# New piece orders, a later place for the first negated copies, and bank drains on VectorE in the units made ahead, in a two-layer hybrid decoder trunk

## The chip, the cores and the metric

The kernel runs on one core of one Trainium2 chip. The metric is the device time of one execution in microseconds; the times of the kernel before and after are medians over several runs. One profiled execution of each kernel gives the trace from which the lines below are taken. Engines are named as in the profile: PE is TensorE (matrix products), PEld its weight loads, DVE is VectorE, ACT is ScalarE, POOL is GpSimd and SP is SyncE, which issues most DMAs.

## The reference

Two decoder layers on 256 tokens of width 2048, all in float32. Cut to what matters:

```python
D_MODEL, SEQ, DEPTH, D_FF = 2048, 256, 2, 8192

def hybrid_layer(x, ...):
    h = rms_norm(x, attn_norm)
    proj = h @ w_in                     # 2048 x 6160: g_q, g_k, g_v, g_gate, g_lr, s_q, s_k, s_v
    log_a = log_sigmoid(g_lr @ w_gate_up + b_gate) / 16
    o_gla = gla_chunked(g_q, g_k, g_v, log_a)            # 8 heads, chunks of 64
    o_gla = rms_norm(o_gla) * silu(g_gate)
    o_sb = stick_breaking_attention(rms_norm(s_q), rms_norm(s_k), s_v)   # 8 heads of 128
    o_sb = rms_norm(o_sb)
    x = x + concatenate([o_gla, o_sb]) @ w_o             # 2048 x 2048
    hm = rms_norm(x, mlp_norm)
    up = square(relu(hm @ w_up))                         # 2048 x 8192
    return x + up @ w_down                               # 8192 x 2048
```

Nearly all of the work is in the products with `w_in`, `w_o`, `w_up` and `w_down`, which are read from DRAM once each. The change touches how these products are ordered and how their results leave the accumulators.

## The kernel before

**Products from high and low parts.** TensorE multiplies a rounded format (`F32R`), so a float32 weight is split: ScalarE rounds it to a high part (`whi`, line L1098), VectorE subtracts that from the weight for the low part (`wlo`, L1102), and every product is three matmuls (`product`, L1231, L1234, L1235): high by high, high by low, low by high. The activations are split in the same way beforehand.

**Units, pieces, steps, banks.** A unit is a product with 2048 rows and 1024 columns of weights. Its rows are cut into 8 pieces of 256 rows, j = 0 to 7; the weights of one piece are one load of 1 MB by SyncE into a `raw` slot (`load`). The unit's order is a list of piece numbers, one number a step: a table such as `EACH` holds the list, the pieces done in the "fast" way and the two "added" pieces. A fast piece has four steps of 6, 6, 6 and 3 matmuls: it forms the 2 x 2 block product with seven products in place of eight, for which VectorE forms sums of weight blocks (`ts`, and sums in place in `raw`, all L876, the line of the helper `combine`). A plain piece has two steps of 12 matmuls. An added piece has two steps of 12, too, but its parts come by DMA: GpSimd issues a load that rounds on its way (`chi`, L1059), ScalarE writes the negated copy of it (`dlo`, L1063, in `negated`), and GpSimd issues a second load that adds the weights to that copy (L1066), which leaves the low part. A unit with four fast pieces has 180 matmuls of 512 columns. Its sums are built in the eight PSUM banks 1 to 8 (tiles `m__...`): in the fast steps 2 and 3, then 5 and 7, then 1 and 6, then 4; in the other steps 2 and 4 with 3 and 8. So banks 5, 7, 1 and 6 are finished with the last fast step, the other four only at the unit's end.

**Slots.** The opening list has six `raw` slots (`FIRST_RAWS`), each later one three (`RAWS`). A load waits until the slot's previous piece has been read for the last time.

**Lists.** The work stands in three planned lists, each followed by work with an order of its own:
- the opening list (`l = -1`): three units made ahead for layer 0's attention, `iv`, `ik`, `iq` (`AHEAD`), ahead of which stands a small opening product (L632, with `copy_first`, L922, that takes its result out of two banks);
- layer 0's list: a gate product, two output units (`o`), sixteen MLP units (four times two `up`, two `down`), and `iv`, `ik`, `iq` for layer 1;
- layer 1's list: gate, two output units, sixteen MLP units.

Ahead of layer 0's and of layer 1's list stands that layer's attention; its first product is the one of L630 to L632 with weights split in L611 and L613, whose first accumulator `acc` takes two banks.

**What sets the order.** `Plan` gets one entry per instruction with its engine, an assumed length, what it depends on and, for loads, an assumed time to landing (`lag`). TensorE's entries stand as the order tables have them; due times for all others follow backwards from them, and a list schedule made with these numbers fixes the program order of ScalarE and VectorE. On the chip each engine works through that order from the front: an instruction that waits holds up all behind it.

**Negated copies at the start.** `rounded` makes the entries of an added piece. For the first three (`CAST`) in the opening list, an entry `held_tile` (L1054) takes the tile by a write of one column, then the load L1059 is issued. The entry `held_tile` has no dependency.

**Tails.** `up_tail` empties the banks of `up` units and of `iv`, `ik`, `iq`. Bank 1 is copied by ScalarE to `box[0]`; VectorE makes `dw` = bank 6 - bank 1, then `y(1, 0)` = bank 5 + `dw`, then `dw` = bank 7 + `dw`; these are the sums. After the last step `half` adds banks 2 and 3 to `y(0, 0)` and `y(1, 0)` on VectorE; banks 4 and 8 are first copied by ScalarE (L1391) into `y(0, 1)` and `y(1, 1)`; VectorE then adds bank 5 once more to the copy of bank 8, and `dw` to both. `relu` (L1410) scales the four results; for `iv`, `ik`, `iq` it is a copy with a factor. `free` holds, for each bank, the entries after which the next unit may write to it.

Of the kernel before, what the change touches and what calls it, by code (L numbers as in the profile page):

```python
# [22 lines left out]
EACH = [0, 0, 1, 1, 1, 2, 7, 3, 3, 3, 3, 2, 5, 5, 5, 5, 4, 1, 6, 6, 6, 4, 6, 7], FAST, (2, 4)  # L23
FEWER = [0, 0, 1, 2, 7, 4, 1, 1, 1, 6, 7, 6, 6, 6, 2, 3, 3, 3, 3, 5, 4, 5], (1, 3, 6), (2, 4)
LATER = [0, 4, 0, 5, 5, 3, 5, 5, 4, 3, 3, 2, 1, 1, 3, 1, 1, 2, 6, 6, 6, 6, 7, 7], FAST, (2, 4)
FAST_OF = {"sxh": (0, 1, 3, 5, 6), "sx": (0, 1, 3, 5, 6)}
TWO_WAYS = (("sxh", 0), ("sx", 0))
O0 = [4, 5, 7, 4, 6, 6, 0, 0, 0, 7, 1, 0, 1, 1, 1, 5, 2, 2, 2, 2, 3, 3], (0, 1, 2), (5, 7)
O1 = [4, 6, 4, 1, 1, 2, 1, 5, 1, 2, 0, 0, 2, 2, 0, 5, 0, 3, 6, 3, 7, 7], (0, 1, 2), (5, 6)
# [3 lines left out]
    ("up", 0): ([2, 5, 5, 5, 5, 1, 1, 1, 1, 2, 0, 0, 0, 3, 4, 0, 3, 3, 3, 6, 4, 6, 6, 6, 7, 7], (0, 1, 3, 5, 6), (2, 4)),  # L33
    ("up", 0, 0): ([0, 0, 3, 4, 3, 3, 1, 3, 4, 1, 1, 1, 5, 5, 2, 5, 5, 6, 6, 2, 6, 6, 7, 7], FAST, (2, 4)),
    ("up", 1): ([7, 7, 5, 5, 4, 5, 5, 1, 1, 1, 2, 3, 1, 3, 3, 3, 4, 6, 6, 6, 6, 0, 2, 0], FAST, (2, 4)),
    ("down", 0): ([0, 0, 1, 1, 1, 3, 4, 1, 3, 5, 3, 3, 4, 5, 5, 5, 2, 6, 6, 6, 6, 7, 7, 2], FAST, (2, 4)),
    ("down", 1): ([7, 7, 3, 3, 4, 3, 3, 5, 5, 5, 4, 5, 1, 1, 1, 1, 0, 0, 2, 0, 0, 6, 6, 6, 6, 2], (0, 1, 3, 5, 6), (2, 4)),
# [137 lines left out]
def trunk_kernel(  # L175
# [275 lines left out]
    def forms(op, i, t, tag):  # L451
# [21 lines left out]
        def high():  # L473
            if e:
# [5 lines left out]
                elif keep:  # L480
                    op.x[i] = act_tile(F32R, (P, 4, 2, P))
                else:
                    op.x[i] = tmp(tag, [P, 3, 2, P], F32R, bufs=len(FAST))
# [375 lines left out]
    def ordered(l, units, hT, rst, ug, gates_t, mixed=None, ons=None):  # L859
# [116 lines left out]
        def turned(n, h2, m, op, key, ll, sums=False):  # L976
# [4 lines left out]
            if sums and i in (FAST if op is hT else FAST_OF["sxh"]):  # L981
# [60 lines left out]
        def rounded(u, j, s):  # L1042
# [27 lines left out]
            if l < 0 and len(chi) < CAST:  # L1070
                first = add("ACT", 0.2, held_tile)
# [167 lines left out]
        def bk(m):  # L1239
            return lambda: banks[m]  # L1240
# [116 lines left out]
        def up_tail(u):  # L1357
# [9 lines left out]

            def new_dw():
# [15 lines left out]
            def half(h, p):  # L1384
                box["r", h] = []
                for tt, m in enumerate(((2, 4), (3, 8))[h]):
                    before = p[m]
                    if tt:
# [7 lines left out]
                    if m == 8:  # L1396
# [569 lines left out]
```

## Time and profile before

| what | value |
|---|---|
| three runs | 2145.78, 2146.07, 2139.18 us |
| median | 2145.78 us |
| the profiled execution | 2145.65 us, of which the trace spans 2144.0 us |
| mean granted TensorE clock of that execution | 0.996 |
| PE, DVE, ACT, POOL busy | 99%, 90%, 70%, 13% |
| DMA over the span | 497.16 MB, 232 GB/s |

The time of an execution is that of the whole run on the device; the span is the part that the trace covers, first to last instruction. The share of busy time counts an engine's own instructions. In the lists of waits the row `A <- B` means that an instruction of A stood idle until B released it; a bracket behind a row of the timeline gives the idle time right ahead of it and what ended it. Names such as `m__230_1143` are tiles, the last number counting through the program.

### The profile page before, as it was taken

How to read it: one execution, taken by the hardware profiler on the slowest of the kernel's cores; microseconds unless marked ns; L12 is line 12 of the kernel's file. 1: busy time of each engine (PE TensorE's matmuls, PEld its weight loads, DVE VectorE, ACT ScalarE, POOL GpSimd, SP SyncE). 2: the span in 40 equal slices, each digit the busy share in tenths (PEclk: the TensorE clock that was granted, in tenths of full speed). 3: DMA queues.
4: the chain of work that ended last, by engine and by line, in shares of the span. 5: the costliest groups of instructions: out<-in, count | busy, mean ns of one | idle time of the engine just before them, and what ended most of it. 6: DMA issues, size and time to landing. Idle time of an engine off the chain costs nothing.

```text
span 2144.0 us, 28336 instructions
## 1 busy us (share of the span) xinstructions
PE 2117.9 (99%) x10040; PEld 1762.7 (82%) x10040; DVE 1936.9 (90%) x2658; ACT 1509.6 (70%) x2044; POOL 279.1 (13%) x394
## 2 busy tenths in 40 slices
PE   8999999999999999999999999999999999999998
PEld 6878888888888888888888888888888888888887
DVE  5887868999999999999998786699999999999998
ACT  6666667777677777668776575677776776786775
POOL 0110001111111111111111000011111111111110
PEclk9999999999999999999999999999999999999999
DMA  8765348788988988987988553678889888889886
GB/s 304 215 192 184 124 136 251 223 251 244 260 258 240 273 255 231 275 261 227 260 252 260 158 173 118 212 220 243 255 253 254 253 259 249 250 256 255 250 246 197
DMA packets 160691, 497.16 MB, mean 232 GB/s; under 512 B 10682, under 2 KB 19458, under 8 KB 160548
## 3 DMA queue, kind: packets, MB, share of 16 engines
q1 hardware_dynamic: 100900, 319.16, 41.3%
q0 software_dynamic: 59648, 176.18, 37.0%
q8 instruction: 79, 1.29, 0.2%
q14 instruction: 64, 0.52, 0.1%
HBM read 493.20 MB, written 2.10 MB: 231 GB/s over the span
## 4 chain that ended last, share of the span: by engine, by line
PE 91%; DVE 3%; ACT 3%; DMA 2%; issue 1%; POOL 0%; ACTq 0%; DVEq 0%
PE acc L630 3%; PE acc L632 3%; PE acc L631 3%; DMA raw<-in_w_in_dram 1%; DVE wlo L1102 1%; ACT whi L611 0%; DMA raw<-in_w_o_dram 0%; ACT whi L1098 0%; DMA chi<-in_w_in_dram 0%; PE ps L1903 0%; DVE wlo L613 0%; PE ps L1896 0%; DVE act L876 0%; PE ps L741 0%; PE ps L1853 0%
## 5 line engine op out<-in xcount | busy, mean ns | idle before, releaser
L1102 DVE TENSOR_TENSOR wlo<-raw,whi 128x1024 fp32r<-128x1024 f32 (+1 forms) x697 | 749.7, 1081 | 75.3 <-ACT whi L1098 41.2
L1098 ACT ACTIVATE whi<-raw 128x1024 fp32r<-128x1024 f32 (+1 forms) x697 | 648.9, 947 | 212.6 <-DVE raw L876 77.8
L1063 ACT ACTIVATE dlo<-chi 128x1024 fp32r<-128x1024 f32 x168 | 177.7, 1058 | 102.1 <-DMA chi<-in_w_in_dram 8.8
L1098 ACT ACTIVATE whi<-ts 128x1024 fp32r<-128x1024 f32 x177 | 187.3, 1058 | 70.0 <-DVE ts L876 33.9
L876 DVE TENSOR_TENSOR ts<-raw 128x1024 f32<-128x1024 f32 x177 | 215.5, 1218 | 11.3 <-DMA raw<-in_w_in_dram 8.6
L1102 DVE TENSOR_TENSOR wlo<-ts,whi 128x1024 fp32r<-128x1024 f32 x177 | 215.3, 1216 | 1.8 <-ACT whi L1098 1.7
L630 PE MATMUL acc<-whi,act 128*128 128x512 f32 (+2 forms) x384 | 142.4, 371 | 4.2 <-DVE act L876 4.2
L611 ACT ACTIVATE whi<-raw 128x1024 fp32r<-128x1024 f32 (+2 forms) x98 | 88.6, 908 | 69.7 <-PE acc L632 66.5
L632 PE MATMUL acc<-whi,act 128*128 128x512 f32 (+2 forms) x384 | 137.7, 359 | 0.0
L631 PE MATMUL acc<-wlo,act 128*128 128x512 f32 (+2 forms) x384 | 137.5, 358 | 0.0
L613 DVE TENSOR_TENSOR wlo<-raw,whi 128x1024 fp32r<-128x1024 f32 (+2 forms) x98 | 100.6, 1031 | 34.8 <-ACT whi L611 34.6
L876 DVE TENSOR_TENSOR raw<-raw 128x512 f32<-128x512 f32 x177 | 121.1, 684 | 1.8
L876 DVE TENSOR_TENSOR raw<-ts,raw 128x512 f32<-128x512 f32 x177 | 120.7, 682 | 0.1
L1059 POOL DMA_DIRECT2D chi<-in_w_up_dram x64 | 38.1, 595 | 515.0 <-PE m__2883_13592 L1235 34.8
L1059 POOL DMA_DIRECT2D chi<-in_w_down_dram x64 | 41.6, 650 | 424.6 <-PE m__914_4357 L1235 22.1
L630 PEld LDWEIGHTS acc<-whi,act 128*128 128x128 f32 x384 | 73.4, 191 | 17.1 <-DVE act L876 5.0
L1066 POOL DMA_DIRECT2D dlo<-in_w_down_dram x64 | 65.3, 1020 | 151.9 <-ACT dlo L1063 123.5
L632 PEld LDWEIGHTS acc<-whi,act 128*128 128x128 f32 x384 | 73.2, 191 | 10.4
L631 PEld LDWEIGHTS acc<-wlo,act 128*128 128x128 f32 x384 | 73.3, 191 | 8.9 <-DVE wlo L613 0.2
L1410 ACT ACTIVATE act<-act,st 128x512 f32<-128x512 f32 x88 | 62.3, 717 | 19.1 <-DVE act L876 18.6
L1066 POOL DMA_DIRECT2D dlo<-in_w_up_dram x64 | 57.9, 905 | 54.8 <-ACT dlo L1063 54.0
L492 DVE TENSOR_TENSOR act<-t,act 128x512 fp32r<-128x512 f32 x94 | 63.6, 682 | 0.0
(4536 smaller groups left out, 5809.3 us busy)
## 6 DMA issues: line engine op xcount, KB each, us to landing
raw<-in_w_up_dram SPq DMA_DIRECT2D x96, 1024.0 KB, 6.8
raw<-in_w_down_dram SPq DMA_DIRECT2D x96, 1024.0 KB, 8.3
raw<-in_w_in_dram SPq DMA_DIRECT2D x72, 1024.0 KB, 7.0
chi<-in_w_up_dram POOLq DMA_DIRECT2D x64, 512.0 KB, 5.2
dlo<-in_w_up_dram POOLq DMA_DIRECT2D x64, 512.0 KB, 7.7
chi<-in_w_down_dram POOLq DMA_DIRECT2D x64, 512.0 KB, 6.1
dlo<-in_w_down_dram POOLq DMA_DIRECT2D x64, 512.0 KB, 8.0
raw<-in_w_o_dram SPq DMA_DIRECT2D x24, 1024.0 KB, 7.7
```

What stands on the lines that cost most here:

```text
L492: nc.vector.tensor_tensor(d[:, :, 1, :], src, f32(d[:, :, 0, :]), ALU.subtract)
L611: newest["hi"] = nc.scalar.activation(h, r, AF.Copy).ins
L613: newest["lo"] = nc.vector.tensor_tensor(lo[:, q : q + step, :width], r, f32(h), ALU.subtract).ins
L630: nc.tensor.matmul(o, xh[:, sl], whi[:, j, :width], start=first, stop=False)
L631: nc.tensor.matmul(o, xh[:, sl], wlo[:, j, :width], start=False, stop=False)
L632: st["mm"] = nc.tensor.matmul(o, xl[:, sl], whi[:, j, :width], start=False, stop=last).ins
L876: nc.vector.tensor_tensor(dst, a, b, op)
L1059: nc.gpsimd.dma_start(flat("h"), src)
L1063: nc.scalar.activation(box["l"], f32(box["h"]), AF.Copy, scale=-1.0)
L1066: nc.gpsimd.dma_start(flat("l"), src, accum_op=ALU.add)
L1098: nc.scalar.activation(box["h"][:, :n], src(), AF.Copy)
L1102: nc.vector.tensor_tensor(box["l"][:, :n], src(), f32(box["h"][:, :n]), ALU.subtract)
```

## The change

It has three parts.

1. All order tables have new lists: of the units made ahead (`EACH` in the opening list; `FEWER` and `LATER` in layer 0's), of the output units (`O0`, `O1`), and of `up` and `down` (`OWN`). The sets of fast and added pieces stay as they are in each. `FAST_OF` gets an entry for `ht` with the value that was used for it before.
2. `held_tile`, the entry ahead of each of the first three casting loads, depends on `before[2]`, one of the five entries that stand for the opening product. That makes `Plan` take these loads, and the negations behind them, as later.
3. In `up_tail`, units made ahead (`not into`) no longer have ScalarE's copies of banks 4 and 8 (two instructions of L1391 less in each of the six units). Bank 7 + `dw` goes straight to `y(0, 1)` in place of `dw`; a new sum right behind it makes `y(1, 1)` = bank 5 + `y(0, 1)`, with the second read of bank 5; banks 4 and 8 are added to these by VectorE from PSUM, bank 4 only after that new sum. `dw` is given back after its last use among the sums. For `up` units only the order of two operands changes.

TensorE has 9826 instructions in both programs, the same of each kind, and VectorE 2660; ScalarE has 2002 in place of 2014. GpSimd's DMAs keep their number; of the 64 casting and 64 adding loads of `w_down`, 16 and 16 change from 512 columns of two row blocks to 1024 columns of one, and 4 and 4 of the 24 and 24 of `w_in` the other way.

```diff
-EACH = [0, 0, 1, 1, 1, 2, 7, 3, 3, 3, 3, 2, 5, 5, 5, 5, 4, 1, 6, 6, 6, 4, 6, 7], FAST, (2, 4)
+EACH = [7, 7, 1, 1, 0, 1, 2, 5, 2, 5, 5, 3, 5, 3, 3, 4, 6, 1, 6, 6, 6, 3, 4, 0], FAST, (2, 4)
-O1 = [4, 6, 4, 1, 1, 2, 1, 5, 1, 2, 0, 0, 2, 2, 0, 5, 0, 3, 6, 3, 7, 7], (0, 1, 2), (5, 6)
+O1 = [4, 5, 4, 2, 2, 2, 2, 6, 1, 1, 0, 0, 1, 1, 0, 0, 6, 5, 7, 7, 3, 3], (0, 1, 2), (5, 6)
...
             if l < 0 and len(chi) < CAST:
-                first = add("ACT", 0.2, held_tile)
+                first = add("ACT", 0.2, held_tile, before[2])
...
+            def dw():
+                return box["w"]
...
                 c = box["c"] = add("ACT", A1, copy, p[1])
                 w = add("DVE", V1, new_dw, c, p[6], take=1, sure=1)
-                a = vector(y(1, 0), bk(5), lambda: box["w"], w, p[5])
-                b = vector(lambda: box["w"], bk(7), lambda: box["w"], w, a, p[7])
+                a = vector(y(1, 0), bk(5), dw, w, p[5])
+                b = vector(dw if into else y(0, 1), bk(7), dw, w, a, p[7])
+                box["s"] = (w, b, a, b)
                 free.update({1: [c], 6: [w], 5: [a], 7: [b]})
-                box["s"] = (w, b, a, b)
+                if not into:
+                    b.give = 1
+                    box["s"] = (w, b, a, vector(y(1, 1), bk(5), y(0, 1), b, p[5]))
+                    free[5] = [a, box["s"][3]]
...
                 for tt, m in enumerate(((2, 4), (3, 8))[h]):
-                    before = p[m]
-                    if tt:
+                    before = [p[m], box["s"][3] if m == 4 and not into else []]
+                    if tt and into:
                         free[m] = before = [add(
                             "ACT", A1,
                             lambda m=m, h=h: nc.scalar.activation(
...
-                    if m == 8:
+                    if m == 8 and into:
                         before = vector(y(1, 1), bk(5), y(1, 1), before, p[5])
                         free[5] = free[5] + [before]
-                    users = box.setdefault("users", []) if tt else []
-                    a = vector(
-                        y(h, tt), y(h, tt), (lambda: box["w"]) if tt else bk(m), before,
-                        box["s"][2 * h + tt], users, op=ALU.subtract if m == 4 else ALU.add,
-                    )
-                    a.give = len(users)
-                    users.append(a)
-                    if not tt:
+                    users = box.setdefault("users", []) if tt and into else []
+                    minus = ALU.subtract if m == 4 else ALU.add
+                    if tt and into:
+                        a = vector(y(h, 1), y(h, 1), dw, before, box["s"][2 * h + 1], users, op=minus)
+                        a.give = len(users)
+                        users.append(a)
+                    else:
+                        a = vector(
+                            y(h, tt), bk(m), y(h, tt), before, box["s"][2 * h + tt], op=minus
+                        )
                         free[m] = [a]
```

What this does to the program order is seen at three places.

ScalarE at the start of the opening list, before. `chi_398`, `chi_400` and `chi_403` are the first three held tiles, `raw_396` the first loaded piece, L922 takes the opening product's result out of its banks:

```order
L1054 ACTIVATE chi_398<-act_304 128x1
L1054 ACTIVATE chi_400<-act_304 128x1
L1054 ACTIVATE chi_403<-act_304 128x1
L1063 ACTIVATE dlo_410<-chi_398 128x1024
L1063 ACTIVATE dlo_414<-chi_400 128x1024
L1098 ACTIVATE whi_74_418<-raw_396 128x1024
L922 ACTIVATE act_382<-acc_145 128x512
L1098 ACTIVATE whi_431<-raw_396 128x1024
```

The same place after:

```order
L1054 ACTIVATE chi_402<-act_304 128x1
L1054 ACTIVATE chi_404<-act_304 128x1
L1054 ACTIVATE chi_407<-act_304 128x1
L1098 ACTIVATE whi_72_412<-raw_396 128x1024
L922 ACTIVATE act_382<-acc_145 128x512
L1098 ACTIVATE whi_421<-raw_396 128x1024
L922 ACTIVATE act_382<-acc_145 128x512
L1098 ACTIVATE whi_443<-raw_398 128x1024
L488 ACTIVATE act_454<-t_73_414 128x4x128
L1098 ACTIVATE whi_466<-ts_452 128x1024
L1063 ACTIVATE dlo_475<-chi_402 128x1024
```

The first two negations (L1063) move from ahead of the first rounding to behind the fourth, and stand apart (the second follows after one more rounding).

VectorE where the unit `ik` ends and `iq` begins, in the opening list, before. `m__177`, `m__172`, `m__158` and `m__165` are the banks 6, 5, 2 and 3 of `ik`, `t_222` is `dw`, `act_1090` and `act_1091` are `box[0]` and `box[1]`; `raw_1011` is piece 1 of `iq`, `raw_859` its piece 0:

```order
L876 TENSOR_TENSOR ts_1093<-raw_1011 128x1024
L876 TENSOR_TENSOR t_222_1103<-m__177_879,act_1090 128x512
L1102 TENSOR_TENSOR wlo_1110<-raw_859,whi_1078 128x1024
L876 TENSOR_TENSOR act_1090<-act_1090,m__158_802 128x512
L876 TENSOR_TENSOR act_1091<-m__172_863,t_222_1103 128x512
L1102 TENSOR_TENSOR wlo_1129<-raw_1011,whi_1098 128x1024
L876 TENSOR_TENSOR act_1091<-act_1091,m__165_830 128x512
```

After. `m__180`, `m__171`, `m__157`, `m__172`, `m__162`, `m__160` and `m__165` are the banks 6, 5, 2, 7, 3, 4 and 8 of `ik`, `raw_852` is piece 7 of `iq` and `raw_1021` its piece 1:

```order
L876 TENSOR_TENSOR t_220_1091<-m__180_893,act_1076 128x512
L1102 TENSOR_TENSOR wlo_1096<-raw_852,whi_1086 128x1024
L876 TENSOR_TENSOR act_1077<-m__171_856,t_220_1091 128x512
L876 TENSOR_TENSOR act_1076<-m__157_797,act_1076 128x512
L876 TENSOR_TENSOR act_1076<-m__172_860,t_220_1091 128x512
L876 TENSOR_TENSOR ts_1124<-raw_1021 128x1024
L876 TENSOR_TENSOR act_1077<-m__171_856,act_1076 128x512
L876 TENSOR_TENSOR act_1077<-m__162_820,act_1077 128x512
L876 TENSOR_TENSOR act_1076<-m__160_810,act_1076 128x512
L876 TENSOR_TENSOR act_1077<-m__165_831,act_1077 128x512
```

Before, every read of these banks stood behind the sum `ts` of the next unit's piece 1. Now those of banks 6, 5, 2 and 7 stand ahead of it; banks 3, 4 and 8 follow right behind it.

VectorE at the end of the opening list, before. `m__242` is bank 5 of `iq`, `m__235` its bank 3, `t_280` is `dw`; L613 and L699 belong to the attention that follows:

```order
L876 TENSOR_TENSOR act_1402<-act_1402,t_280_1408 128x512
L876 TENSOR_TENSOR act_1403<-act_1403,m__235_1168 128x512
L613 TENSOR_TENSOR wlo_1536<-raw_1533,whi_1535 128x2x272
L699 TENSOR_REDUCE st_1529<-t_307_1551 128x4
L876 TENSOR_TENSOR act_1403<-m__242_1201,act_1403 128x512
```

After. `m__229`, `m__241`, `m__230`, `m__233` and `m__236` are the banks 2, 5, 4, 3 and 8:

```order
L876 TENSOR_TENSOR act_1395<-m__229_1140,act_1395 128x512
L876 TENSOR_TENSOR act_1396<-m__241_1197,act_1395 128x512
L613 TENSOR_TENSOR wlo_1482<-raw_1463,whi_1481 128x2x272
L876 TENSOR_TENSOR act_1395<-m__230_1151,act_1395 128x512
L291 CAST ident_292_1497<-ident 128x128
L306 CAST tri_1499<-t_298_1508 128x128
L876 TENSOR_TENSOR act_1396<-m__233_1164,act_1396 128x512
L308 CAST nones_1500<-t_299_1509 128x128
L699 TENSOR_REDUCE st_1523<-t_303_1524 128x4
L876 TENSOR_TENSOR act_1396<-m__236_1175,act_1396 128x512
```

The second read of bank 5 was VectorE's last read of any bank of `iq`; now it comes ahead of the reads of banks 4, 3 and 8.

More of the change, by code (lines that the diff above doesn't have):

```diff
@@ L32 @@
 OWN = {
[L33 to L37, printed above, removed]
+    ("up", 0): ([2, 6, 6, 6, 6, 3, 3, 3, 3, 4, 1, 1, 5, 1, 2, 1, 5, 5, 5, 0, 4, 0, 0, 0, 7, 7], (0, 1, 3, 5, 6), (2, 4)),
+    ("up", 0, 0): ([0, 0, 1, 4, 1, 1, 5, 1, 5, 2, 3, 5, 3, 3, 5, 2, 3, 6, 6, 6, 6, 4, 7, 7], FAST, (2, 4)),
+    ("up", 1): ([0, 0, 3, 3, 4, 3, 3, 5, 5, 5, 6, 5, 2, 6, 6, 6, 1, 1, 2, 1, 1, 7, 4, 7], FAST, (2, 4)),
+    ("down", 0): ([0, 0, 3, 3, 1, 4, 3, 3, 1, 5, 1, 2, 1, 5, 5, 5, 2, 6, 6, 6, 6, 4, 7, 7], FAST, (2, 4)),
+    ("down", 1): ([7, 7, 3, 3, 2, 3, 3, 1, 1, 1, 2, 1, 0, 0, 0, 0, 5, 5, 4, 5, 5, 6, 6, 6, 6, 4], (0, 1, 3, 5, 6), (2, 4)),
 }
@@ L482, in high @@
                 else:
[L483 removed]
+                    op.x[i] = tmp(tag, [P, 3, 2, P], F32R, bufs=4)
                 todo.append((op.x[i], e[0]))
@@ L980, in turned @@
             a = add("PE", 4 * TR, turn, x_done[n], free[m])
-            if sums and i in (FAST if op is hT else FAST_OF["sxh"]):
+            if sums and i in FAST_OF["ht" if op is hT else "sxh"]:
                 box = []
```

8 lines of the change are left out of this document (4 added, 4 removed).

## The prediction

> **What bounds the kernel now.** The first view is the page's busy times, the second the list of waits of TensorE (engine and line waiting, released by; total, times, longest), the third TensorE's timeline (start, length, and in brackets the idle time before).
>
> ```profile
> span 2144.0 us, 28336 instructions
> ...
> PE 2117.9 (99%) x10040; PEld 1762.7 (82%) x10040; DVE 1936.9 (90%) x2658; ACT 1509.6 (70%) x2044; POOL 279.1 (13%) x394
> ```
>
> ```profile
> PE m__86_446 L1231 <- ACT whi L1098: 8.1, 1, 8.1
> PE m__230_1143 L1231 <- DVE act L876: 4.2, 1, 4.2
> PE acc L630 <- DVE act L876: 4.2, 2, 2.7
> ```
>
> ```profile
> 33.68 0.39 PE L632 MATMUL acc<-whi,act 128*128 128x512 f32 x1
> 42.20 0.79 PE L1231 MATMUL m__86_446<-whi,act 128*128 128x512 f32 x1 [8.13 <-ACT whi L1098]
> ...
> 47.74 0.40 PE L1235 MATMUL m__87_447<-whi,act 128*128 128x512 f32 x1
> ...
> 127.31 0.39 PE L1235 MATMUL m__167_840<-whi,act 128*128 128x512 f32 x1
> 131.90 0.47 PE L1231 MATMUL m__230_1143<-whi,act 128*128 128x512 f32 x1 [4.21 <-DVE act L876]
> ...
> 132.93 0.63 PE L1234 MATMUL m__230_1143<-wlo,act 128*128 128x512 f32 x1
> ...
> 136.32 0.39 PE L1231 MATMUL m__235_1168<-whi,act 128*128 128x512 f32 x1
> ...
> 174.18 0.39 PE L1235 MATMUL m__238_1179<-whi,act 128*128 128x512 f32 x1
> 176.04 0.39 PE L630 MATMUL acc<-whi,act 128*128 128x272 f32 x1 [1.47 <-DVE act L876]
> ...
> 1205.65 0.39 PE L1235 MATMUL m__2269_10677<-whi,act 128*128 128x512 f32 x1
> ...
> 1207.69 0.39 PE L1235 MATMUL m__2271_10683<-whi,act 128*128 128x512 f32 x1
> 1210.77 0.39 PE L630 MATMUL acc<-whi,act 128*128 128x272 f32 x1 [2.69 <-DVE act L876]
> ...
> 1211.51 0.43 PE L632 MATMUL acc<-whi,act 128*128 128x272 f32 x1
> ...
> 1214.91 0.29 PE L632 MATMUL acc<-whi,act 128*128 128x272 f32 x1
> ```
>
> TensorE is busy 99% of the span, and the change neither adds nor removes a matmul (the instruction lists of both kernels hold the same PE rows, reordered). So it can win only where TensorE stands, and lose only by making it stand. A matmul of 512 columns starts every 0.227 us (nine starts from 1205.65 to 1207.69). Against that spacing the timeline gives four gaps:
> - A, start of the opening list: 42.20 - 33.68 - 0.23 = 8.29 lost. The next 11 starts take until 47.74, 5.54 instead of 2.50: the clock had fallen to half and one low part came late. 3.04 more, 11.3 in all.
> - B, between ik and iq of that list: 131.90 - 127.31 - 0.23 = 4.36. From 132.93 to 136.32 eight starts take 3.39 instead of 1.81, which with 0.1 ahead of them is 1.7. In all 6.1.
> - C, end of that list: 176.04 - 174.18 - 0.23 = 1.6, and no slow stretch behind it.
> - D, end of layer 0's list: 1210.77 - 1207.69 - 0.23 = 2.85. From 1211.51 to 1214.91, 15 starts of 272 columns take 3.40, where 15 at 0.227 x 272/512 = 0.12 would take 1.8. About 1.5 more, 4.35 in all.
>
> Together 23.4 us, 1.1% of the run, and most that can be had. [...]
>
> **Gap A: the negated copies move back on ScalarE.** Rows of ScalarE, then VectorE, then GpSimd:
>
> ```profile
> 29.82 0.48 ACT L1054 ACTIVATE chi<-act 128x1 fp32r<-128x1 f32 x3
> 37.76 1.06 ACT L1063 ACTIVATE dlo<-chi 128x1024 fp32r<-128x1024 f32 x1 [7.46 <-DMA chi<-in_w_in_dram]
> 40.14 1.06 ACT L1063 ACTIVATE dlo<-chi 128x1024 fp32r<-128x1024 f32 x1 [1.32 <-DMA chi<-in_w_in_dram]
> 41.10 1.04 ACT L1098 ACTIVATE whi<-raw 128x1024 fp32r<-128x1024 f32 x1
> 42.05 0.58 ACT L922 ACTIVATE act<-acc 128x512 f32<-128x512 f32 x1
> ...
> 42.18 1.23 DVE L1102 TENSOR_TENSOR wlo<-raw,whi 128x1024 fp32r<-128x1024 f32 x1 [12.72 <-ACT whi L1098]
> ...
> 39.12 0.89 POOL L1066 DMA_DIRECT2D dlo<-in_w_in_dram  x1 [6.89 <-ACT dlo L1063]
> ```
>
> ScalarE reaches the two negations at 30.30 and stands there until their loads land at 37.8 and 40.1. The first rounding, whose own load it did not have to wait for, is queued behind them. In the new order that rounding comes next after L1054. I walk the queues with these durations (ACT 1.04, or 0.95 start to start; DVE 1.23; L922 0.58). Rounding 1: 30.3 to 31.3, its low part to 32.6, ahead of TensorE's 33.91. L922 waits for the last matmul of the opening unit (33.68 + 0.39) and ends at 34.7; rounding 2 to 35.7, its low part to 37.0. TensorE does a step of 12 matmuls in 2.72 and wants that part at 36.86: 0.15 late. Rounding 3 to 37.2; the sum `ts` on VectorE to 38.5, low part 3 to 39.7, wanted at 39.7; rounding 4 to 39.6. Steps 3 and 4 lose another 0.4 or so in the same way: call it 0.6.
>
> What is late next is the low part made by the adding load. The negation now stands behind rounding 4: 39.5 to 40.6, its chi having landed at 37.8, so nothing queues behind a load here. GpSimd issued 0.30 after the negation's end before (38.82 to 39.12), so at 40.9 instead of 39.1; its three chi loads keep their place. The page has the landings:
>
> ```profile
> raw<-in_w_in_dram SPq DMA_DIRECT2D x72, 1024.0 KB, 7.0
> ...
> dlo<-in_w_in_dram POOLq DMA_DIRECT2D x24, 512.0 KB, 8.0
> ```
>
> With 8.0 it lands at 48.9. TensorE wants it at step 6, after steps of 12, 12, 6, 6, 12, 6 matmuls: 33.91 + 54 x 0.227 + 0.23 + 0.6 = 47.0. That is 1.9 of new wait. Bounds: 0 if it lands as fast as the raw loads' 7.0 with a microsecond of slip elsewhere, 8 if it takes what the slowest raw load below takes. I take 1.9, since the median is of this very load. A: 11.3 - 0.6 - 1.9 = **8.8 gained** (3 to 11.3).
>
> **Gap B: drains and the order inside the opening list.** The chain of waits gives the load, VectorE's timeline what it held up:
>
> ```profile
> 113.42 14.76 DMA raw<-in_w_in_dram
> ...
> 128.20 1.23 DVE L876 TENSOR_TENSOR ts<-raw 128x1024 f32<-128x1024 f32 x1 [7.45 <-DMA raw<-in_w_in_dram]
> ...
> 131.08 0.68 DVE L876 TENSOR_TENSOR act<-act,m__158_802 128x512 f32<-128x512 f32 x1
> ```
>
> The sum `ts` of piece 1 waited for a load of 14.76 us, and the drains of ik's banks, queued behind it on VectorE, kept bank 2 (m__158) from iq's first matmul. In the new order the drains of banks 6, 5, 2 and 7 stand ahead of that `ts`, and 33 matmuls (7.5 us) instead of 15 (3.4 us) lie between the slot released before piece 1's and its own, so its load shares the queue with less. I take B's 6.1 as gone. Not gone for free: bank 4 is now drained on VectorE behind bank 3, which TensorE finishes 6 matmuls (1.4 us) before the unit's end. Two drains of 0.68 end 0.2 after the end or so, and the next unit wants bank 4 another 1.4 us later. If VectorE is more than 1.2 us behind, that is a new wait.
>
> The price is piece 0. Its second step is now the last of the unit, its slot is released there, and the next unit wants the new load at step 4, 36 matmuls (8.2 us) after the boundary. The roundings ran 3.8 us ahead of TensorE there (slot freed and the load issued at 79.61 in the row below, its step due at 83.4 after 168 of the unit's 180 matmuls, which end at 86.1). So from issue to landing there are 3.8 + 2.7 + 8.2 less 2.3 for rounding and low part, 12.4 us.
>
> ```profile
> 79.61 15.12 DMA raw<-in_w_in_dram
> ```
>
> Against the median of 7.0 that is enough; against 15.12 and 14.76, the two loads of this list that the chain names, 2.7 and 2.4 are missing, at ik and at iq. No row tells which holds; both are in this same list, the median is mostly of others. I take half, 1.3 each. B: 6.1 - 2.6 = **3.5 gained** (-1 to 6.1).
>
> **Gaps C and D: the lists' ends.**
>
> ```profile
> 1209.42 0.57 ACT L1391 ACTIVATE act<-m__2271_10683 128x512 f32<-128x512 f32 x1
> ...
> 1210.02 0.69 DVE L876 TENSOR_TENSOR act<-m__2278_10722,act 128x512 f32<-128x512 f32 x1
> ```
>
> ScalarE copied bank 8 after the last matmul, then VectorE added bank 5 (m__2278) to the copy, and TensorE started at 1210.77 as bank 5 came free; the attention's first accumulator lies in banks 5 and 7. The change reads bank 5 twice right after the sums, which need no bank of the last two steps (24 matmuls, 5.4 us). Bank 5 is free before the list ends, and the first weights of the attention are ready in all rows above (TensorE was released by VectorE's drain). C and D go: **6.0 gained** (4 to 6.0, if a late drain of another bank takes 1 us at each end).
>
> **The drains themselves.** Twelve ScalarE copies of 0.57 go (two in each of six units), 7 us of an engine busy 70%: nothing on the path. VectorE keeps eight drains a unit; two of them per unit now read PSUM that did not.
>
> ```profile
> L876 DVE TENSOR_TENSOR act<-act,t x52: 676/683/693, 104.0 to 2058.5; 128x512 f32<-128x512 f32 x52
> ...
> L876 DVE TENSOR_TENSOR act<-act,m__86_446 x1: 680/680/680, 82.9 to 82.9; 128x512 f32<-128x512 f32 x1
> ```
>
> 683 ns from SBUF, 680 with a bank: no cost. [...]
>
> **The other orders.** In the lists of layers 0 and 1 TensorE hardly waits, so new orders there can only lose. A raw slot serves every third load. Counted in the tables, the matmuls between a slot's last step and the first step of its next load were never under 51 (11.6 us) in the output and MLP units. Now 14 pieces (piece 1 of each first down unit, piece 5 of three first up units a layer) have 48 (10.9 us), and piece 4 of the second output unit has 42 (9.5 us) in both layers. Less 2.3 for rounding, 8.6 and 7.2 are left for the load.
>
> ```profile
> raw<-in_w_down_dram SPq DMA_DIRECT2D x96, 1024.0 KB, 8.3
> ...
> ACT whi L1098 <- DMA raw<-in_w_o_dram: 2.9, 1, 2.9
> ```
>
> 8.3 fits in 8.6, barely; ScalarE already waited 2.9 once for an output weight without TensorE waiting, so some lead hides more. I take **2 lost** (0 to 10). The wider rows of 16 of the 64 casting down loads, and of their adding ones, change a transfer that no wait above names: nothing.
>
> **Sum.** 8.8 + 3.5 + 6.0 - 2 = 16.3 off the profiled execution's 2145.65 (span 2144.0 and 1.65 around it), which lies within 0.1% of the median 2145.78: 2129.
>
> **Rivals.**
> - The wait of A only changes its name: the adding load, issued later, takes the 14.8 of the slow loads, lands at 55.7, and TensorE stands 8.7 with 1.6 of half clock behind. Speaks for it: TensorE's raw loads run at the same time. Against: its median of 8.0. A then gives 0.4 and the time is 2137.5.
> - Piece 0 lands late at both boundaries by 4 us, with the half clock behind each: 2 x 5.6 instead of 2.6 lost, 2138. For it: the two 15 us loads. Against: they had four others around them.
> - Slower: slot reuse in the layers. If the 14 pieces' loads land after 10.5 instead of 8.3 us, each stands 1.9, 27 us in all, and the time is 2145.65 - 18.3 + 27 = 2154. It outweighs the gains from 1.3 us a piece, a landing of 9.9. For it: DMA moves 230 GB/s all the time; against: the waits of ScalarE up to 2.9 that never reached TensorE.
> - The change does nothing: the pauses at the lists' ends and at the boundary come from VectorE being late as a whole, not from the bank named; then only A counts: 2137 to 2146.
>
> **How the numbers follow.** The forecast's own case holds 0.66 (2122, all gaps gone, to 2135); the first rival 0.09, the second 0.11, slower 0.07, nothing 0.07. The range for 8 in 10 runs from 2120 to 2140, up to the first two rivals. About 0.3%, 6.4 us, is what a measurement here can tell from no change (the three runs of before lie 0.3% apart). Under 2139.3 fall the forecast, most of the two next rivals (0.17 of 0.20) and a third of the last: 0.85; within 0.3%: 0.08; slower: 0.07.
>
> **What would show it.** In the waits of TensorE after: no wait for `whi` of 8 us at the first list, but one of 1 to 2 us for a `dlo` load; no wait of `acc` L630 for VectorE over 1 us; in place of the 4.2 at iq's start, waits of up to 2.5 us four steps into ik and iq for the roundings of piece 0. The clock stays whole around 1211. ScalarE loses 12 rows. Wrong would be a TensorE wait in the MLP units that recurs with every down or up unit, or waits of over 3 us in the opening list.

## The result, and the profile after

The changed kernel takes 2122.68 us (median of four runs, 2121.85 to 2123.87) where the kernel before takes 2144.51 (2139.18 to 2146.07). The ratio is 0.9903, with a 95% interval of 0.9884 to 0.9922. The forecast was 2129 with a range of 2120 to 2140. By these medians the gain is 21.8 us. The profiled execution took 2122.05, 23.6 less than that of before; the tables below go by profiled executions.

The page's span and busy times, then the waits of TensorE (all rows):

```profile
span 2120.2 us, 28343 instructions
...
PE 2111.3 (100%) x10040; PEld 1758.5 (83%) x10040; DVE 1936.9 (91%) x2658; ACT 1498.6 (71%) x2032; POOL 273.6 (13%) x394
```

```profile
PE ps L580 <- POOL ident masks.py:199: 1.4, 1, 1.4
PE ps L741 <- DVE act L704: 1.1, 2, 0.5
PE ps L507 <- DMA xb<-in_x_dram: 0.5, 1, 0.5
PE m__1856_8735 L1438 <- DVE act L876: 0.2, 1, 0.2
```

All three waits of before that stood behind the gaps A to D are gone, and none of the waits that the prediction put in their place is there: none for `dlo`, none for the roundings of piece 0. TensorE's timeline at the four places (from the opening product to the first unit; from `ik` to `iq`; at the ends of the opening list and of layer 0's list):

```profile
33.44 0.39 PE L632 MATMUL acc<-whi,act 128*128 128x512 f32 x1
33.66 0.39 PE L1231 MATMUL m__83_436<-whi,act 128*128 128x512 f32 x1
...
115.80 0.39 PE L1235 MATMUL m__165_831<-whi,act 128*128 128x512 f32 x1
116.02 0.39 PE L1231 MATMUL m__229_1140<-whi,act 128*128 128x512 f32 x1
...
156.60 0.39 PE L1235 MATMUL m__236_1175<-whi,act 128*128 128x512 f32 x1
156.82 0.28 PE L630 MATMUL acc<-whi,act 128*128 128x272 f32 x1
...
1188.51 0.39 PE L1235 MATMUL m__2275_10694<-whi,act 128*128 128x512 f32 x1
1188.73 0.28 PE L630 MATMUL acc<-whi,act 128*128 128x272 f32 x1
```

Each pair starts 0.22 apart, the plain spacing of two matmuls.

The next table applies the prediction's measure to the profiled execution of every kernel below: the distances between the starts of TensorE's matmuls, less 0.2268 for each 512 columns, summed over the stretch, with the half clock behind a pause included (granted clock 0.50 from 1211.5 to 1214.5 in the kernel before). "Layers" is all that is lost in the units of layers 0 and 1, in many small pauses.

| kernel | A, first unit | between units of the opening list (B) | C | D | layers |
|---|---|---|---|---|---|
| before | 11.3 | 6.6 | 1.6 | 4.5 | 6.1 |
| changed | 0.7 | 0 | 0 | 0 | 6.2 |
| held_only | 3.3 | 0 | 1.6 | 4.5 | 5.7 |
| tail_only | 10.6 | 5.1 | 0 | 0 | 6.6 |
| each_only | 11.2 | 0 | 1.6 | 4.6 | 5.8 |
| old_each | 3.1 | 1.2 | 0 | 0 | 6.7 |
| late_start | 15.4 | 0 | 1.6 | 4.3 | 6.1 |
| no_tail | 0.8 | 0 | 1.6 | 2.1 | 6.1 |
| late_bank5 | 0.7 | 1.1 | 2.2 | 4.0 | 6.2 |
| old_layers | 1.6 | 0 | 0 | 0 | 6.0 |
| no_held | 11.0 | 0 | 0 | 0 | 5.8 |
| held_later | 8.0 | 0 | 0 | 0 | 7.0 |
| zero_early | 2.6 | 1.9 | 0 | 0 | 6.3 |
| early_neg | 11.9 | 0 | 1.6 | 4.5 | 6.1 |

From before to changed the sum falls by 24.0 - 0.7 = 23.3 in A to D, which is all but 0.3 of the 23.6.

Each row is one execution. The kernel before varies most: its 52 runs here lie between 2137.94 and 2147.92 with a median of 2143.03, and its profiled one, 2145.65, is among the longer. By medians held_only gains 11.9 and each_only 4.0, where their rows say 15.0 and 6.9. The shortest runs of before are as short as those of each_only (2137.33 to 2139.59), which has no gap B. So B, seen in the traces of before and tail_only, may be smaller or absent in other executions of these two; no trace shows one.

### The profile page after: what moved, and what is told of

Read it like the earlier page. It is cut to its first block, busy times and chain, and to the rows that moved or that the text cites. A ratio compares the mean times of both kernels' runs of the same rounds, so it can differ in the third digit from the quotient of the medians.

```text
span 2120.2 us, 28343 instructions
## 1 busy us (share of the span) xinstructions
PE 2111.3 (100%) x10040; PEld 1758.5 (83%) x10040; DVE 1936.9 (91%) x2658; ACT 1498.6 (71%) x2032; POOL 273.6 (13%) x394
## 4 chain that ended last, share of the span: by engine, by line
PE 76%; issue 17%; POOL 2%; DVE 1%; DMA 1%; ACT 1%; POOLq 0%; ACTq 0%
PE acc L630 3%; PE acc L632 3%; PE acc L631 3%; POOL dlo L1066 1%; POOL chi L1059 1%; DMA raw<-in_w_up_dram 1%; DMA dlo<-in_w_down_dram 1%; DVE wlo L613 0%; PE ps L741 0%; PE ps L759 0%; PE ps L1912 0%; ACT whi L611 0%; DVE t L1767 0%; PE ps L1862 0%; PE ps L795 0%
## 5 line engine op out<-in xcount | busy, mean ns | idle before, releaser
L1063 ACT ACTIVATE dlo<-chi 128x1024 fp32r<-128x1024 f32 x168 | 177.7, 1058 | 106.5 <-DMA chi<-in_w_down_dram 12.7
L613 DVE TENSOR_TENSOR wlo<-raw,whi 128x1024 fp32r<-128x1024 f32 (+2 forms) x98 | 100.4, 1031 | 30.0 <-ACT whi L611 29.2
L1066 POOL DMA_DIRECT2D dlo<-in_w_down_dram x64 | 59.6, 931 | 127.8 <-ACT dlo L1063 121.6
```

Source lines behind the costliest of these rows:

```text
L613: newest["lo"] = nc.vector.tensor_tensor(lo[:, q : q + step, :width], r, f32(h), ALU.subtract).ins
L1063: nc.scalar.activation(box["l"], f32(box["h"]), AF.Copy, scale=-1.0)
L1066: nc.gpsimd.dma_start(flat("l"), src, accum_op=ALU.add)
```

## The experiments

"part 1" is the tables, "part 2" `held_tile`'s dependency, "part 3" `up_tail`. Every kernel was run beside the kernel before on the same chip; ratios are to that.

**One part alone: held_only.** The kernel before with

```diff
-                first = add("ACT", 0.2, held_tile)
+                first = add("ACT", 0.2, held_tile, before[2])
```

> The kernel before with the later place of the first negated copies alone (part 2). My theory, that each gap of TensorE has its own cause and this part owns gap A alone: A shrinks from 11.3 to 0.7, the wait of 8.1 for the rounding (whi L1098) at the first unit is gone, gaps B (4.2, half clock behind), C (1.5) and D (2.7) stay as they were, and the time is 2145.65 - 10.6 = 2135. Rival 1, the wait only changes its name: a wait of 2 to 9 for the adding load (dlo) stands in the first unit, 2137 to 2145. Rival 2, TensorE being 10 earlier makes the slow loads of the opening list later for it: B grows by several us and the time is 2138 to 2143.

Measured: 2130.56, ratio 0.9945 (0.9924 to 0.9966). Its waits of TensorE:

```profile
PE acc L630 <- DVE act L876: 4.2, 2, 2.7
...
PE m__83_436 L1234 <- DMA dlo<-in_w_in_dram: 1.0, 1, 1.0
PE m__81_434 L1234 <- DVE wlo L1102: 0.8, 1, 0.8
```

A fell to 3.3, not to 0.7: in the old order TensorE wants the first added piece 12 matmuls earlier and waits 1.0 for its adding load, and there are two small waits for low parts (0.8 and 0.4). And B is gone, which no theory had, so the theory of one cause for each gap fell. The pauses of C and D stayed to the hundredth (1.47 and 2.69).

**One part alone: tail_only.** The kernel before with the new `up_tail`.

> The kernel before with the drains on VectorE and the early second read of bank 5 alone (part 3). My theory: C and D go (1.6 and 4.35), A stays at 11.3; at B the drains still stand behind the sum ts of the next unit's piece 1 in VectorE's order, so B stays at 6.1: 2145.65 - 6.0 = 2139.7. Rival 1, the pauses come from VectorE being late as a whole: C and D move by under 1 and the time is 2145. Rival 2, the direct drains and not the order free B as well: 2133.6.

Measured: 2136.25, ratio 0.997 (0.996 to 0.998). C and D are gone, A stays. At B the drains still stand behind the sum `ts`, and two waits of 1.2 and 1.8 in place of one of 4.2 leave 5.1 of 6.6. That is as the theory had it, with B a little smaller. The profiled execution was 2138.12, 7.5 below that of before; the medians differ by 6.2.

**One part alone: each_only.** The kernel before with the line `EACH` of the changed kernel.

> The kernel before with the new order of the opening list's units alone (EACH). My theory: the drains of banks 6, 2 and 5 stand ahead of the sum ts, so B (6.1) is gone; A (11.3), C (1.6) and D (4.35) stay: 2145.65 - 6.1 = 2139.5. Rival 1: the loads of 15 in this list come with the slots, whatever the order; the ts is late all the same and TensorE waits for its rounding or for piece 0 instead: B or a new wait of 2.5 to 6, 2143 to 2146. Rival 2: the order also changes what TensorE needs first at the start, and A changes by more than 2.

Measured: 2138.47, ratio 0.9978 (0.9966 to 0.999). B is gone, A, C and D stand as before, as the theory had it, although the load issued at 80.44, for `ik`, right behind that of piece 0, still takes 14.4:

```profile
raw<-in_w_in_dram SPq DMA_DIRECT2D x1, 1024.0 KB, 14.4
```

So the order alone closes B as well, and in the changed kernel B has two remedies, each enough without the other.

**One part undone: old_each.** The changed kernel with the line `EACH` of before.

> The changed kernel with the old order of the opening list's units (EACH of before), everything else changed. My theory: B comes back with its wait of about 4 and the half clock behind it, A, C and D stay closed: 2122.7 + 6.1 = 2128.8. Rival 1: the drains on VectorE or the earlier start free B by themselves, 2122.7. Rival 2: with A closed TensorE runs 10 earlier against the same loads and B is larger than before, 2131 to 2135.

Measured: 2126.41, ratio 0.993 (0.9904 to 0.9956). B comes back with only 1.2 (a wait of 0.9 for bank 4, which the next unit wants from its seventh matmul on and which is now drained behind a low part), A grows by 2.4 to 3.1 and one wait of 0.5 for an adding load of a `down` unit appears. B's 6.1 did not come back, so the theory fell here too: rival 1 is nearer.

**What opened B: late_start.** held_only with copies without use ahead of ScalarE's first rounding:

```diff
+                held.append(box["h"])
+                if len(held) == CAST:
+                    for _ in range(23):
+                        nc.scalar.activation(box["h"][:, 0, :], xb[3][:, 1, :], AF.Copy)
```

> The kernel before with the later place of the first negated copies, and 23 ScalarE copies of 128x512 without use (into a tile whose load follows) ahead of ScalarE's first rounding, so that the rounding starts near 41 as it did in the kernel before, with no negation ahead of it. It asks why gap B (4.2 of wait at the start of iq) was gone when only the start was mended. Theory, the late start itself: ScalarE and VectorE catch up through the first unit, release their slots closer together, the loads that follow crowd each other (15.1 and 14.8 in the kernel before, 11.2 and 10.9 with the start mended), and the sum ts waits for its load: with the late start B comes back with 3 to 6, loads of over 13 stand in the list again, and A is 9 to 12: about 2130.6 + 8 + 5 = 2143 to 2147. Rival, the place of the negations and of their adding loads in the queues made B: B stays closed, only A comes back, 2138 to 2140.

Measured: 2142.45 (one run). TensorE waited 12.4 at the start, longer than meant, and nowhere between the units. That is held_only's 2130.56 and some 12 for the start. So a late start alone does not open B, as far as one execution can tell; that theory fell.

**What opened B: early_neg.** held_only with the first two negations put back ahead of the first rounding, in the code that emits the program and not in the plan. ScalarE's rows then differ from held_only's in these two alone, and no other engine's differ:

```diff
                 nc.gpsimd.dma_start(flat("h"), src)
+                if l < 0 and len(early) < 2:
+                    early.append(negated)
...
             def high():
+                while l < 0 and len(early) == 2 and first_two:
+                    first_two.pop()
+                    for f in early:
+                        f()
```

> The kernel before with the later place of the first negated copies, so with the program order that this gives to all engines, but with its first two negations (L1063) put back by hand ahead of ScalarE's first rounding, as in the kernel before; nothing else moves on any engine. It asks what opened gap B in the kernel before, now that a late start by dummy copies did not. Theory 1, the order that the plan gives to the rest of the first unit when it takes the negations early (roundings, sums and the third to fifth negations stand otherwise) crowds the loads: here that order is the new one, so A comes back (8.1 of wait, 11.3 in all, in place of 3.0) and B stays closed: 2130.6 + 8.3 = 2139. Theory 2, the early negations with their early adding loads do it themselves, whatever the order of the rest: A and B come back, loads of 15 among them, 2144 to 2146.

Measured: 2138.95, ratio 0.9985 (0.9975 to 0.9995), as theory 1 had it. TensorE's wait at the start is back, B is not. The two loads that the chain of before named took 15.1 and 14.8; the loads in their places here (issued at 79.71 and 111.03), and VectorE's wait for the second of them, before 7.45:

```profile
raw<-in_w_in_dram SPq DMA_DIRECT2D x1, 1024.0 KB, 11.3
raw<-in_w_in_dram SPq DMA_DIRECT2D x1, 1024.0 KB, 10.8
...
DVE ts L876 <- DMA raw<-in_w_in_dram: 0.8, 1, 0.8
```

With the old `EACH`, what is left as B's cause is the program order of the rest of the first unit, as the plan makes it when it takes the negations early: the third to fifth negation, sums and roundings stand otherwise in ScalarE's and VectorE's first hundred rows. Which of these rows delays the loads is open, and it rests on one trace of each kernel.

**The lists' ends: no_tail.** The changed kernel with the `up_tail` of before.

> The changed kernel with the tail of before (bank copies on ScalarE, second read of bank 5 last). Theory, each list's end has its own cause: C and D come back as in the kernel before (1.6, and 2.85 with 1.5 of half clock), A and B stay closed: 2122.7 + 6.0 = 2128.7. Rival, VectorE being late as a whole makes the pauses: with the start mended and the new orders they come back at under half, 2124 to 2125.

Measured: 2129.62, ratio 0.9937 (0.992 to 0.9954), as the theory had it. The profiled execution, 2125.84, was the shortest of four (the others 2129.24 to 2131.17): D was a pause of 1.8 without half clock behind it (granted clock 1.00 from 1192 to 1195); the last section compares such pauses.

**The lists' ends: late_bank5.** The changed kernel with banks 4 and 8 drained on VectorE as in it, but bank 5's second read last:

```diff
-                b = vector(dw if into else y(0, 1), bk(7), dw, w, a, p[7])
+                b = vector(dw, bk(7), dw, w, a, p[7])
...
+                        if m == 8 and not into:
+                            a = vector(y(1, 1), bk(5), y(1, 1), a, p[5])
+                            free[5] = free[5] + [a]
```

> The changed kernel with banks 4 and 8 drained on VectorE as in it, but with the second read of bank 5 last again, behind the drain of bank 8 (dw is kept until then). Theory, the place of bank 5's second read made C and D: both come back, each about 1.6 (0.7 for bank 8 and 0.7 for bank 5 behind the last matmul), D up to 4.35 if the pause passes into half clock: 2125.5 to 2128.5. Rival, ScalarE's copies in the path made them: no pause over 0.5, 2122.7.

Measured: 2130.9, ratio 0.9947 (0.993 to 0.9963). Both pauses are back, and larger than in no_tail, which has ScalarE's copies (2.07 and 2.16 against 1.45 and 1.82), and 1.1 is lost near the start of `ik`, for the low part of piece 0. VectorE and TensorE at the end of the opening list:

```profile
157.62 0.39 PE L1235 MATMUL m__236_1174<-whi,act 128*128 128x512 f32 x1
160.07 0.36 PE L630 MATMUL acc<-whi,act 128*128 128x272 f32 x1 [2.07 <-DVE st L411]
...
158.04 0.69 DVE L876 TENSOR_TENSOR act<-m__236_1174,t 128x512 f32<-128x512 f32 x1
158.65 0.68 DVE L699 TENSOR_REDUCE st<-t 128x4 f32<-128x512 f32 x1
159.24 0.68 DVE L876 TENSOR_TENSOR act<-m__241_1197,act 128x512 f32<-128x512 f32 x1
```

Bank 5 (`m__241`) is read until 159.92 and `acc` starts 0.15 later; the bracket names the instruction after that read. So the place of bank 5's second read makes C and D, and taking ScalarE's copies away brings nothing by itself. In the changed kernel that read starts 3.2 ahead of the list's last matmul (153.36 against 156.60):

```profile
153.36 0.68 DVE L876 TENSOR_TENSOR act<-m__241_1197,act 128x512 f32<-128x512 f32 x1
```

**The layers' orders: old_layers.** The changed kernel with all tables but `EACH` as before.

> The changed kernel with the old orders in the lists of layers 0 and 1 (FEWER, LATER, O0, O1 and the five of up and down), EACH new. The prediction had 2 lost (0 to 10) to slots that come free later for their next load under the new orders. By it this kernel takes 2120.7. Theory after the first runs, loads land with room in these lists either way: no change, 2122 to 2123.5. Rival, the new orders gain there: 2124 to 2126, with small waits of 0.3 to 0.7 in the layers' units as the kernel with the old EACH showed two.

Measured: 2122.95 (five runs, 2122.61 to 2124.6), ratio 0.9912 (0.9896 to 0.9927), where the changed kernel has 2122.68 and 0.9903. There is no change that can be told, and the layers' pauses sum to 6.0 against 6.2.

**no_held.** The changed kernel without `held_tile`'s dependency.

> The changed kernel with the early negations of before (held_tile without its dependency), new orders and new tail kept. Theory after the first runs, A comes back whole (11.3 against 0.7) and B stays closed by the new order alone, C and D by the tail: 2122.7 + 10.6 = 2133.3. Rival, the planned order behind the early negations crowds the loads (15 in three kernels that had them) and opens B again in spite of the new order: 2136 to 2139.

Measured: 2132.27, ratio 0.9943 (0.9926 to 0.996), as the theory had it: A is back with 11.0, B stays closed by the new order.

**The room of the adding load: held_later.**

```diff
-                first = add("ACT", 0.2, held_tile, before[2])
+                first = add("ACT", 0.2, held_tile, before[4])
```

> The changed kernel with held_tile depending on before[4] in place of before[2]: ScalarE now takes the tiles behind its third rounding, GpSimd issues the casting loads near 37 in place of 30, and the negations stand behind three more roundings. It measures how much room the negation's path has. Theory: casting load landed at 44 to 46, negation to 45.3, adding load issued at 45.6 and landed after 5.8 to 8.0 at 51.4 to 53.6, TensorE wants it at 46.9: a wait of 4.5 to 6.7 for dlo or chi in the first unit, up to 1.6 of half clock: 2127 to 2131. Rival, the early loads crowded each other and land faster when issued later: 2123 to 2125.

Measured: 2129.68, ratio 0.9929 (0.9913 to 0.9946). The adding load was issued at 45.47 and took 5.9; TensorE waited 4.7 for it and ran at half clock behind (mean granted clock of the execution 0.998, where the changed kernel has 1.000):

```profile
PE m__80_428 L1234 <- DMA dlo<-in_w_in_dram: 4.7, 1, 4.7
...
dlo<-in_w_in_dram POOLq DMA_DIRECT2D x1, 512.0 KB, 5.9
```

That is as the theory had it: 5.1 later in issue than in the changed kernel (40.41) costs 7.0.

**The room of piece 0's load: zero_early.**

```diff
-EACH = [7, 7, 1, 1, 0, 1, 2, 5, 2, 5, 5, 3, 5, 3, 3, 4, 6, 1, 6, 6, 6, 3, 4, 0], FAST, (2, 4)
+EACH = [7, 7, 0, 1, 1, 1, 2, 5, 2, 5, 5, 3, 5, 3, 3, 4, 6, 1, 6, 6, 6, 3, 4, 0], FAST, (2, 4)
```

> The changed kernel with EACH beginning 7, 7, 0, 1, 1, 1, 2 in place of 7, 7, 1, 1, 0, 1, 2: the next unit wants piece 0, whose slot is released at the end of the unit before, 12 matmuls (2.7) earlier. It measures the room of that load. In the changed kernel at iq the load was issued at 109.15, ScalarE's rounding of it began at 120.20, its low part ended at 122.5, and TensorE wanted it at 124.4: 1.9 of room. Theory: 2.7 - 1.9 = 0.8 of wait at iq, and up to as much at ik: 2123.5 to 2124.5. Rival, the prediction's loads of 15 in this place: 3 to 5 of wait at each of the two, 2129 to 2133. Rival 2, the order planned from the table takes it up: 2122.7.

Measured: 2126.57, ratio 0.9913 (0.9893 to 0.9933). A miss in the sizes: nothing was lost at `iq`, 1.9 at `ik` (waits of 0.2 and 0.8 for a rounding and its low part, with what follows them), and 1.9 more in the first unit, where the planned order changed too. Piece 0's loads took 10.0 and 10.8, not 15; rival 1 fell.

## Why the prediction was right, and where its terms were off

**What bounds it: right.** The prediction said that the change can win only where TensorE stands. The four gaps held 23.4 by its count, 24.0 by the table's, and closing them took 23.6 off the profiled execution (21.8 by the medians). The median came out 6.7 below the sum (2145.65 - 16.3 = 2129.35): the gains at A and B were put too low, and the loss charged to the other orders did not come. All three errors go the same way, so none hid another.

**Gap A: mechanism right, gain too small by 1.8.** 10.6 came against 8.8. The walk through the queues (0.6 of small losses) met 0.7. The term that was mis-sized is "what is late next", the 1.9 for the adding load. ScalarE's negation and GpSimd's issue, in the trace after, with the landing:

```profile
39.06 1.04 ACT L1063 ACTIVATE dlo<-chi 128x1024 fp32r<-128x1024 f32 x1
40.41 0.89 POOL L1066 DMA_DIRECT2D dlo<-in_w_in_dram  x1 [8.40 <-ACT dlo L1063]
...
dlo<-in_w_in_dram POOLq DMA_DIRECT2D x1, 512.0 KB, 5.8
...
46.89 0.39 PE L1234 MATMUL m__83_436<-dlo,act 128*128 128x512 f32 x1
```

Issued at 40.41 against 40.9 forecast, landed after 5.8 against 8.0, so at 46.2; TensorE used it at 46.89 with 0.7 to spare. The 8.0 was the median of all 24 adding loads of that weight; the same first load in the kernel before, a row that the prediction did not use, had taken 6.0. held_later shows that the step itself was sound: 5.1 later in issue, and TensorE waits for just this load. The room of 0.7 is also why the new order belongs to part 2: with the old one (held_only, old_each) the load is wanted earlier and costs 1.0 and 0.8.

**Gap B: closed, but not for the reason given alone, and its price was nothing.** 6.6 came against 3.5. That the new order closes B is shown by each_only and no_held. The prediction gave two reasons, the drains ahead of `ts` and more time for the load that `ts` needs. Both hold in the trace after: there `ts` stands behind four drains and waits for nothing, as its load, issued at 101.66, had landed at 109.10.

```profile
113.33 0.68 DVE L876 TENSOR_TENSOR act<-m__172_860,t 128x512 f32<-128x512 f32 x1
113.93 1.21 DVE L876 TENSOR_TENSOR ts<-raw 128x1024 f32<-128x1024 f32 x1
```

No run has the one without the other, so which of them does it is not shown. That the order inside the list was needed was wrong: part 2 closes B without it (held_only), where the two loads in the places of the slow ones took 11.2 and 10.9. The term that failed is "half, 1.3 each" for piece 0's load at `ik` and `iq`. At `iq`, with SyncE's issue, ScalarE's rounding, VectorE's low part and TensorE:

```profile
106.59 3.72 SPq L1023 DMA_DIRECT2D raw<-in_w_in_dram  x3
...
120.20 2.96 ACT L1098 ACTIVATE whi<-raw 128x1024 fp32r<-128x1024 f32 x3 [1.87 <-DMA raw<-in_w_in_dram]
121.29 1.23 DVE L1102 TENSOR_TENSOR wlo<-raw,whi 128x1024 fp32r<-128x1024 f32 x1 [0.29 <-ACT whi L1098]
...
124.41 0.39 PE L1234 MATMUL m__229_1140<-wlo,act 128*128 128x512 f32 x1
```

The load is the second of the three issues, at 109.15, and it landed at 120.09, as ScalarE waited for it until 120.20: 10.9, inside the 12.4 that the prediction had counted as room, between its 7.0 and its 15. At `ik` piece 0's load took 9.7. Loads of 15 have not gone from the list: by the trace's landings the load issued right behind piece 0's took 14.8 at `ik` (issued at 70.23) and 16.0 at `iq` (109.57), and in each_only, without part 2, 14.4 and 15.9 beside 8.6 and 11.0 for piece 0. But that load is for piece 3, which TensorE wants only at the unit's twelfth step. So the prediction charged piece 0 with the landing of other loads. Its count of the room was nearer: in late_bank5 piece 0's load at `ik` took 12.3, and 1.1 was lost there.

**Gaps C and D: right.** 6.0 was forecast, and it is 6.1 by the table (1.6 and 4.5). late_bank5 shows that the reason was the right one. About 1.6 of D is half clock, and in the runs a pause in that place had it behind (2.16 in late_bank5) or not (1.82 in no_tail), by where the pause fell (last section): there the count on one execution was partly luck.

**The drains: right.** Bank 4 read by VectorE in the trace after takes what the sums from SBUF took before (683 ns):

```profile
116.26 0.68 DVE L876 TENSOR_TENSOR act<-m__160_810,act 128x512 f32<-128x512 f32 x1
```

**The other orders: 2 lost was forecast, nothing was lost.** The step that failed sets a room of 8.6 against a median landing of 8.3 and charged 2 for it: in old_layers the layers' pauses are the same. ScalarE waits more for `up` weights after the change, as its list of waits shows (after, then before), and less for `down` weights (10.3 before, no such row after), and none of it reaches TensorE:

```profile
ACT whi L1098 <- DMA raw<-in_w_up_dram: 13.3, 16, 1.7
```

```profile
ACT whi L1098 <- DMA raw<-in_w_up_dram: 5.1, 7, 1.3
```

The slot count says when a load can start; whether TensorE waits depends on the lead of the roundings as well, which the prediction named and then did not count.

**The half clock.** The prediction counted half speed behind D's pause of 2.69, as the rows of before have it. The runs bear the rows out: in all five traces with a pause of 2.69, 3.41 of half clock followed, and in tail_only 1.83 of idle time was enough. The last section has the numbers.

## What to carry to other kernels

Where one engine sets the time and is busy 99% of it, list the places where it stands, find for each the one instruction that ends the wait, and ask what is queued ahead of that on its engine: here a load's wait ahead of unrelated roundings, a sum that waits for a load ahead of bank drains, and one late second read of a bank. A bank that the next stage opens with should be read for the last time first, before anything that waits for the last matmul. When a price is charged for a load, take the landings of that load in that place, not a median over the program nor those of its neighbours, and subtract the lead that its consumer has; parts that share a planner's schedule do not add up, so try each alone and each undone.

## What the runs showed that was not expected

**What halves the clock.** Over all profiled executions here, single pauses of TensorE of 1.45 to 2.07 (nine of them) were followed by full speed, and those of 2.16 (one) and 2.69 (five) by 3.41 of half clock. In late_bank5 one of each stands in one execution; the columns are the window and its length, the busy times of PE, PEld, DVE, ACT and POOL with counts, the granted clock, the DMA share and GB/s:

```profile
160.00:163.00 3.00, 2.93 (x23) 2.96 (x24) 2.48 (x8) 1.65 (x4) 0.00 (x0) 1.00 0.34 78
1194.00:1197.00 3.00, 3.00 (x15) 3.00 (x15) 2.33 (x7) 0.52 (x2) 0.48 (x2) 0.50 0.45 153
```

The first follows the pause of 2.07, the second that of 2.16. In these traces it went by where a pause fell, and not by its length alone. In every trace the stretches of half clock start whole multiples of 3.413 apart and last one or more such steps (the last runs into the program's end); in the kernel before they start at 37.29, 132.86 and 1211.48, 28 and 316 steps apart. Add up TensorE's idle time in each step of this grid, from 12 us on, over all fourteen traces. Each of the 28 steps at full clock with 1.83 or more of idle time was followed by a step at half clock, and none of those with 1.75 or less was. Five pauses as examples:

| pause of TensorE | idle time in the steps that it touches | clock in the step after each |
|---|---|---|
| late_bank5, C, 2.07 | 1.33 and 0.74 | full, full |
| late_bank5, D, 2.16 | 2.14 and 0.02 | half, full |
| no_tail, D, 1.82 | 0.49 and 1.33 | full, full |
| tail_only, B, 1.19 | 1.19 | full |
| tail_only, B, 1.83 | 1.83 | half |

So in these traces a pause of about 2 us cost its length alone (1.82, 2.07) or a stretch of half clock as well (1.83, 2.16), by where the grid lay, and the grid of one trace is not that of another: in the kernel before a stretch starts at 37.29, in the changed kernel at 2118.80, 609.8 steps later. Whether that makes the times of one kernel differ between executions was not measured.

**A plan's side effect.** With the old `EACH`, a dependency meant for three small instructions changed the order of ScalarE's and VectorE's first hundred rows, and with it the landing of loads issued some 40 and 75 us later (15.1 and 14.8 in the kernel before, 11.3 and 10.8 in early_neg with the same early negations). For part 2 alone the table has 6.6 us of this at B, beside 8.0 at A, but the medians show only 11.9 of these 14.6 us. With the new `EACH` no such effect on the loads is seen: in no_held, with the early negations, the loads of piece 0 and of piece 3 behind it took 9.4 and 16.0 at `ik`, and in the changed kernel 9.7 and 14.8.
